# 192 tokens instead of 128 gather expert rows, and the first feed-forward layer runs in two passes

## The chip, the cores and the metric

One core of a Trainium2 chip runs the whole program. The metric is device time in microseconds (us) of one execution. The kernel before took 3000.18 us (median of three runs, 2999.29 to 3005.09). A difference of 0.2% is 6 us.

## What is computed

Two transformer layers on 512 tokens of width 1024, in float32. The parts that the change touches are the second half of the first layer and the first feed-forward layer of the second:

```
# product-key experts: 8 heads, each chooses 16 of 16384 experts per token
s1, i1 = top_k(scores of key half 1, 16);  s2, i2 = top_k(scores of key half 2, 16)
top_s, pos = top_k(s1[:, None] + s2[None, :], 16);  idx = (i1 * 128 + i2)[pos]
g = softmax(top_s)
act = gelu(einsum('thkd,td->thk', u_tab[idx], h))       # u_tab, v_tab: 16384 x 1024
x = x + einsum('thk,thkd->td', g * act, v_tab[idx])

# first feed-forward layer of the second block, 2816 hidden columns
x = x + 0.5 * ((silu(h2 @ w_gate) * (h2 @ w_up)) @ w_down)
```

Ahead of this stands an attention and recurrent block, behind it a second mixing block and a second feed-forward layer. Neither is changed.

## The kernel before

Activations lie transposed, channels on partitions and tokens along the free axis; `x` is eight tiles of 128 x 512. Every large product is made of three matmuls (`mm3`, lines 234 to 236): weights and activations are split into a high part in the fast float32 form and a low remainder, and high x high, low x high and high x low are added up in PSUM. A chunk of weights (128 x 1024, 512 KB) is loaded by SP into `wraw`, rounded by ScalarE into `whi` (L212), and subtracted by VectorE, or by GpSimd where `pool_lo` says so, into `wlo` (L213). One chunk feeds eight `mm3`, which is 24 matmuls.

`phase_b` computes the experts in two ways. The tokens 0 to `TG`-1 (128 before) gather the rows of the experts that they chose: GpSimd issues an indirect DMA for one row of every token (L884, 128 rows of 4 KB, 512 KB in one issue), and VectorE takes the dot product with the token's activations (`u` rows, L895) or adds the weighted row to an accumulator (`v` rows, L902). There are 128 choices per token and two tables, hence 256 such issues. The other `ND` tokens (384) go through all 16384 experts as products: 128 `u` tiles (`u_tile`, 8 `mm3` each), then 32 groups of `v` products (`v_group`, 4 chunks of 8 `mm3`), weighted by a dense table of gates that is zero where a token did not choose an expert.

The stages follow one another in time:

* **Routing** (`side`, `u_spill`). VectorE picks the best keys of each block of 128 tokens (`choose`, four times). For blocks 1 to 3 the gates of 4 tokens at a time are built: one-hot tiles `ohA`, `ohB` by VectorE, ScalarE and GpSimd (L852 to L863), a product per token (L838), a copy (L839), and a DMA to DRAM per 32 tokens. Beside this `SPILL` = 68 of the 128 `u` tiles are computed and spilled to DRAM.
* **Experts** (`main`). The other 60 `u` tiles and all `v` groups, with the gates (`gt`) and the spilled tiles (`gr`) read back, multiplied by VectorE or GpSimd in turn (L959), split (L962, L963), used, and the results added to `x` (L974).
* **First feed-forward layer** (`ffn`). 44 chunks up (gate and up columns for 22 hidden tiles) and 8 products of 22 `mm3` down, on all 512 tokens.

The generator `weave` sets the order: it emits a list `a` and beside it as much of a list `b` as a ratio of estimated costs allows; once `b` is done, a third list `c` may take its place. `u_spill` is woven with `side` (ratio `RR`), which emits the routing and with it `GR` parts of gather, and the gather itself is the third list. `main` is woven with the rest of the gather (ratio `VR`). Each gather issue and each use is held back (`pace`) until a matmul that stands ahead of it in that order is done, so the gather keeps step with TensorE. At most `ROWB`-1 = 3 rows are under way ahead of their use. Engines run their own queues in program order.

Of the kernel before, what the change touches and what calls it, by code (L numbers as in the profile page):

```python
# [25 lines left out]
C_IND, C_M1024, C_M128, C_M256, C_INVF, C_O256 = 832, 834, 835, 836, 837, 838  # L26
NCONST = 966
# [25 lines left out]
AR = 1.4        # paces: projections over attention, in both blocks  # L53
MR = 1.8
MO = 2          # query tile after which the memory's keys and values follow
SO = 0.5        # shift of the spilled groups among the others
BC = 1200       # cost of building the gates of 4 tokens
PJ = 15         # first expert tiles, whose low parts are left to Pool


def make_consts():
# [21 lines left out]
    c[:, C_O256:C_O256 + 128] = 1.0 / 256  # L83
    return c
# [33 lines left out]
class Norm:  # L118
# [33 lines left out]
    def finish(self, bc=True):  # L152
        k, nc = self.k, self.k.nc
        nb = self.n // 128
        ps = k.ps("st")
        for b in range(nb):
            nc.tensor.matmul(ps[:, b:b + 1], self.acc[:, b * 128:(b + 1) * 128], k.cst(C_M1024, 1),
                             start=True, stop=True)
        v = k.tiny.tile([128, nb], F32, name="nv")
        nc.vector.tensor_scalar(v, ps[:, :nb], EPS, None, op0=OP.add)  # L160
        self.rn = k.tiny.tile([128, nb], F32, name="nrn", bufs=3)
        k.rsqrt(v, self.rn)
        if bc:
            self.bc = k.tmp.tile([128, self.n], F32, name="nbc", bufs=2)
            pb = k.ps("T")
            for b in range(nb):
                nc.tensor.transpose(pb[:, b * 128:(b + 1) * 128], self.rn[:, b:b + 1].to_broadcast([128, 128]),
                                    k.ident)
            nc.scalar.activation(self.bc, pb[:, :self.n], AF.Copy)


class Kern:
# [44 lines left out]
    def pace(self, ins, back=1):  # L217
        """Hold ins, which is ready long before its turn, until a late matmul traced so far."""
# [4 lines left out]
    def flush(self):  # L223
        """What waits for the end of the last projection, traced some products into the next one."""
# [33 lines left out]
    def bcast_nat(self, f):  # L258
        """f(b) -> [128 tokens, 128] AP whose columns follow the output partitions."""
# [6 lines left out]
    # ------------------------------------------------------------------ setup  # L266
# [15 lines left out]
    def late_setup(self):  # L282
# [13 lines left out]
        # lambda of the differential attention  # L296
# [9 lines left out]
        # 4 * softplus(-rg_lambda)  # L306
# [20 lines left out]
    # ------------------------------------------------------------------ block 1  # L327
    def phase_a(self):
# [104 lines left out]
        # ---- differential attention  # L433
# [24 lines left out]
        def kq_pair(p):  # L458
            """Keys (normed) and raw queries of heads 2p, 2p+1; the queries' factors in FQ."""
# [196 lines left out]
        # ---- out projection and residual  # L656
# [22 lines left out]
    # ------------------------------------------------------------------ product-key experts  # L679
    # Tokens 0..TG-1 gather the rows of their experts; the others go through all experts as matrix  # L680
    # products, weighted by their gates (zero where a token did not choose an expert).
    def phase_b(self, n2):
        nc, I, x = self.nc, self.I, self.x
        ACT, V, G = nc.scalar, nc.vector, nc.gpsimd
        ND = T - TG
# [15 lines left out]
        hnat = gp_.tile([128, 1024], F32, name="hnat")  # L701
        hhi, hlo = [], []
        ph = None
        for hc in range(16):
# [9 lines left out]
            if hc % 2 == 1:  # L714
# [9 lines left out]
                if k % 4 == 0:  # L724
                    ph = self.ps("L")
                nc.tensor.transpose(ph[:, (k % 4) * 128:(k % 4) * 128 + 128], t[:, :TG], self.ident)
                if k % 4 == 3:
                    ACT.activation(hnat[:, (k // 4) * 512:(k // 4) * 512 + 512], ph, AF.Copy)
# [14 lines left out]
        gsel0 = gp_.tile([128, 8, 16], F32, name="gsel0")  # L743
        eidx = gp_.tile([128, 128], I32, name="eidx")

        eidx_done = []
# [36 lines left out]
            # position -> (r1, r2): the candidates run row by row, rows 0..7 of 16 // (r + 1), then ones  # L783
# [37 lines left out]
        def routing():  # L821
# [4 lines left out]
            for b in (1, 2, 3):  # L826
                gsel, sel = yield from choose(b)
                pt = self.ps("T")
# [6 lines left out]
                def build(stg, t0, t1, A, B):  # L835
# [5 lines left out]
                    if t1 == t0 + 28:  # L841
                        nc.sync.dma_start(Gd[(b - 1) * 4 + t0 // 32].rearrange("p j t -> p (j t)"),
                                          stg.rearrange("p j t -> p (j t)"))

                for t0 in range(0, 128, 32):
# [25 lines left out]
        def gather():  # L871
            """Tokens 0..127: dot products with the gathered rows of peer_u, then the weighted sum of peer_v's."""
            g2 = gsel0.rearrange("p h s -> p (h s)")
            acc = gp_.tile([128, 1024], F32, name="gacc")
            V.memset(acc, 0.0)
            dots = gp_.tile([128, 128], F32, name="dots")
            junk = gp_.tile([128, 1024], F32, name="junk")
            seq = [(tab, s) for s0 in range(0, 128, 16) for tab in "uv" for s in range(s0, s0 + 16)]
            rows = {}

            def issue(n):
                tab, s = seq[n]
                rows[n] = gp_.tile([128, 1024], F32, name="row", bufs=ROWB)
                self.pace(G.indirect_dma_start(out=rows[n], out_offset=None, in_=I[tab + "_nat"],  # L884
                                               in_offset=bass.IndirectOffsetOnAxis(ap=eidx[:, s:s + 1], axis=0)))

            for n in range(ROWB - 1):
                issue(n)
                yield 1170
            for n, (tab, s) in enumerate(seq):  # L890
                if n + ROWB - 1 < len(seq):
                    issue(n + ROWB - 1)
                row = rows.pop(n)
                if tab == "u":
                    self.pace(V.scalar_tensor_tensor(junk, row, 1.0, hnat, op0=OP.mult, op1=OP.mult,  # L895
# [7 lines left out]
                yield 1170  # L903
            for k in range(2):
                pt = self.ps("T")
                for q in range(4):
                    m = 4 * k + q
                    nc.tensor.transpose(pt[:, q * 128:(q + 1) * 128], acc[:, m * 128:(m + 1) * 128], self.ident)
                for q in range(4):
                    m = 4 * k + q  # L910
                    V.tensor_tensor(x[m][:, :TG], x[m][:, :TG], pt[:, q * 128:(q + 1) * 128], op=OP.add)
# [12 lines left out]
        def u_spill():  # L924
            for j in range(SPILL):
                yield from u_tile(j, rp, True)

        gat = gather()

        def side():  # L930
            c0 = c1 = 0.0
            for c in routing():
# [3 lines left out]
                while c1 < c0:  # L936
                    c = next(gat)
                    c1 += c
# [663 lines left out]
```

## Time and profile before

| | |
|---|---|
| median of three runs | 3000.18 us |
| lowest, highest | 2999.29, 3005.09 us |
| span of the profiled execution, first to last instruction | 2996.1 us |
| median above that span | 4.1 us |
| TensorE busy | 2865.3 us (96%) |
| VectorE, ScalarE, GpSimd busy | 2062.3, 1216.5, 822.9 us |
| bytes moved by DMA | 494.07 MB, 165 GB/s over the span |

The profiled execution has no time of its own beside its span; the fastest run lies 3.2 us above it. The table's shares are means over stages with different limits: the slices show a stretch in the middle, from slice 16 to 26, in which the DMA engines are at nine tenths, and a stretch from slice 10 on in which VectorE is.

### The profile page before, as it was taken

Reading aid. Unit: us, or ns where it says so; the run is one execution under the profiler, and the core shown is the slowest. Engines: PE = TensorE matmul, PEld = TensorE weight load, DVE = VectorE, ACT = ScalarE, POOL = GpSimd, SP = SyncE. Lnnn points to the kernel's source line nnn. Section 1 sums busy time; section 2 is a strip of 40 time slices with the busy share of each in tenths; the row PEclk is TensorE's granted clock in tenths of the full one; section 3 lists DMA queues with packets and bytes.
Section 4 is the critical chain, followed back from the end, with each engine's and each line's share of the span. In section 5 each row is a group of like instructions: output and inputs, shape, how many; then the busy total and the mean of one; then the engine's idle time right before and its main releaser. Section 6 shows DMA issues by size and latency. Waiting matters only on the chain. (4 is left out here: it accounts for less than half of the span.)

```text
span 2996.1 us, 39620 instructions
## 1 busy us (share of the span) xinstructions
PE 2865.3 (96%) x14551; PEld 2486.6 (83%) x14551; DVE 2062.3 (69%) x3978; ACT 1216.5 (41%) x1893; POOL 822.9 (27%) x633
## 2 busy tenths in 40 slices
PE   8899999999789998999999999999999999999999
PEld 6578777788789898899999999997888866678887
DVE  5763466679998967898898888995443477454432
ACT  4652344333365756333333333343222355632221
POOL 1320000000486968454544444520000022000000
PEclk9999999999999999999999999999999988999999
DMA  4123211332366767999998998962223321123232
GB/s 161 57 71 106 78 50 50 103 102 84 126 209 229 240 231 282 324 309 314 312 315 297 311 316 287 318 214 92 99 97 92 99 66 39 53 92 99 96 103 76
DMA packets 189250, 494.07 MB, mean 165 GB/s; under 512 B 16000, under 2 KB 84736, under 8 KB 187392
## 3 DMA queue, kind: packets, MB, share of 16 engines
q1 hardware_dynamic: 152192, 357.31, 35.8%
q0 software_dynamic: 36864, 134.23, 13.3%
q8 instruction: 115, 1.88, 0.3%
q14 instruction: 79, 0.65, 0.1%
HBM read 450.84 MB, written 40.63 MB: 164 GB/s over the span
## 5 line engine op out<-in xcount | busy, mean ns | idle before, releaser
L212 ACT ACTIVATE whi<-wraw 128x1024 fp32r<-128x1024 f32 (+1 forms) x526 | 547.2, 1041 | 1247.2 <-PE mm L235 600.1
L234 PE MATMUL mm<-hhi,whi 128*128 128x512 f32 (+1 forms) x2368 | 895.1, 378 | 30.1 <-ACT gs L918 17.0
L236 PE MATMUL mm<-hhi,wlo 128*128 128x512 f32 (+1 forms) x2368 | 882.1, 372 | 5.9 <-DVE wlo L213 5.8
L235 PE MATMUL mm<-hlo,whi 128*128 128x512 f32 (+1 forms) x2368 | 883.1, 373 | 0.0
L213 DVE TENSOR_TENSOR wlo<-wraw,whi 128x1024 fp32r<-128x1024 f32 (+1 forms) x491 | 605.9, 1235 | 274.6 <-ACT whi L212 272.4
L234 PEld LDWEIGHTS mm<-hhi,whi 128*128 128x128 f32 x2368 | 451.5, 191 | 89.7 <-ACT gs L918 17.9
L236 PEld LDWEIGHTS mm<-hhi,wlo 128*128 128x128 f32 x2368 | 451.0, 190 | 65.9 <-DVE wlo L213 9.6
L235 PEld LDWEIGHTS mm<-hlo,whi 128*128 128x128 f32 x2368 | 452.1, 191 | 53.3 <-issue 2.9
L884 POOL DMA_INDIRECT row<-v_nat,eidx x128 | 174.3, 1361 | 176.5 <-PE mm L236 47.6
L884 POOL DMA_INDIRECT row<-u_nat,eidx x128 | 169.3, 1323 | 160.0 <-PE mm L236 40.9
L863 POOL TENSOR_SCALAR ohB<-consts,sT 128x128 f32<-128x128 f32 x192 | 204.1, 1074 | 25.4 <-ACT sT L832 22.0
L902 DVE SCALAR_TENSOR_TENSOR gacc<-row,dots,gacc 128x1024 f32<-128x1024 f32 x128 | 173.8, 1358 | 14.3 <-PE mm L236 6.2
L895 DVE SCALAR_TENSOR_TENSOR junk<-row,hnat 128x1024 f32<-128x1024 f32 x128 | 165.0, 1289 | 17.6 <-DMA row<-u_nat,eidx 6.0
L213 POOL TENSOR_TENSOR wlo<-wraw,whi 128x1024 fp32r<-128x1024 f32 x35 | 89.2, 2549 | 320.1 <-ACT whi L212 319.8
L838 PE MATMUL L<-ohA,ohB 128*128 128x128 f32 x768 | 115.1, 283 | 25.1 <-POOL ohB L863 17.5
L234 PE MATMUL mm<-fhi,whi 128*128 128x512 f32 x352 | 139.1, 395 | 0.0
L236 PE MATMUL mm<-fhi,wlo 128*128 128x512 f32 x352 | 139.0, 395 | 0.0
L235 PE MATMUL mm<-flo,whi 128*128 128x512 f32 x352 | 139.0, 395 | 0.0
L838 PEld LDWEIGHTS L<-ohA,ohB 128*128 128x128 f32 x768 | 102.7, 192 | 37.1 <-POOL ohB L863 29.7
L1039 DVE TENSOR_TENSOR fu<-mm,nbc 128x512 f32<-128x512 f32 x44 | 30.4, 692 | 141.7 <-PE mm L236 141.7
L839 ACT ACTIVATE stg<-L 128x512 f32<-128x512 f32 x96 | 106.6, 1115 | 46.0 <-PE L L838 45.7
L1193 POOL MEMSET cvh<- 128x30 f32 x2 | 0.3, 126 | 382.8 <-DVE fu L1040 276.0
(2360 smaller groups left out, 5032.2 us busy)
## 6 DMA issues: line engine op xcount, KB each, us to landing
wraw<-u SPq DMA_DIRECT2D x128, 512.0 KB
wraw<-pv SPq DMA_DIRECT2D x128, 512.0 KB
gates<-stg SPq DMA_DIRECT2D x12, 2048.0 KB
gt<-gates SPq DMA_DIRECT2D x32, 768.0 KB
spill<-gs SPq DMA_DIRECT2D x68, 192.0 KB
gr<-spill SPq DMA_DIRECT2D x68, 192.0 KB
wraw<-w_f1g SPq DMA_DIRECT2D x22, 512.0 KB
wraw<-w_f1u SPq DMA_DIRECT2D x22, 512.0 KB
```

What stands on the lines that cost most here:

```text
L212: nc.scalar.activation(hi[:, :n], raw[:, :n], AF.Copy)
L213: (nc.gpsimd if pool_lo else nc.vector).tensor_tensor(lo[:, :n], raw[:, :n], hi[:, :n].bitcast(F32), op=OP.subtract)
L234: nc.tensor.matmul(ps, a[0], b[0], start=start, stop=False)
L235: nc.tensor.matmul(ps, a[0], b[1], start=False, stop=False)
L236: self.mms.append(nc.tensor.matmul(ps, a[1], b[0], start=False, stop=stop).ins.name)
L838: nc.tensor.matmul(gp[:, q * 128:(q + 1) * 128], B[:, q], A[:, q], start=True, stop=True)
L839: ACT.activation(stg[:, :, t1 - t0:t1 - t0 + 4].rearrange("p j t -> p t j"), gp.rearrange("p (t j) -> p t j", t=4), AF.Copy)
L863: G.tensor_scalar(B[:, q], iota, sT[:, 128 + tt:129 + tt], None, op0=OP.is_equal)
L884: self.pace(G.indirect_dma_start(out=rows[n], out_offset=None, in_=I[tab + "_nat"], in_offset=bass.IndirectOffsetOnAxis(ap=eidx[:, s:s + 1 ...
L895: self.pace(V.scalar_tensor_tensor(junk, row, 1.0, hnat, op0=OP.mult, op1=OP.mult, accum_out=dots[:, s:s + 1]), BACK)
L902: self.pace(V.scalar_tensor_tensor(acc, row, dots[:, s:s + 1], acc, op0=OP.mult, op1=OP.add), BACK)
L1039: V.tensor_tensor(u, pu, n.bc, op=OP.mult)
```

## The change

`TG` becomes 192. The first 128 gathering tokens are handled as before. The 64 others lie twice on the 128 partitions: the upper half of the partitions handles the choices 64 to 127 of the same tokens. So they need 64 choices x 2 tables = 128 further issues of 128 rows. Their activations (`hnat[1]`), expert numbers (`eidx1`) and gates (`gsel1`) are put there by small products, and the two halves of their result are added by a product with the stacked unit matrix `C_STK`. The products of `phase_b` then stream `ND` = 320 columns, not 384; ten, not twelve, blocks of 32 tokens get gates. 84 tiles are spilled, not 68. Once the routing has been emitted, the gather goes on beside the rest of `u_spill` at ratio `RR` = 1; what is left of it is spread evenly over the experts and over the up products of the first feed-forward layer.

That layer runs in two passes: `ffn_up` on the 320 tokens inside the weave, `ffn_down` on them, and then the whole layer again on the 192 gathering tokens, with all its weights loaded and split a second time. More low parts go to GpSimd: every third `u` tile after the spilled ones too, one chunk in eight of the `v` products, and every second `up` chunk of the two passes.

```diff
-SPILL = 68      # expert tiles whose activations wait in DRAM until the gates are there
-TG = 128        # tokens that gather their experts' rows
+SPILL = 84
+TG = 192
+TX = TG - 128
+XR = 128 // TX
+ND = T - TG
+MMC = 440
-VR = 0.345
+GC = 1170
...
-                    ph = self.ps("L")
-                nc.tensor.transpose(ph[:, (k % 4) * 128:(k % 4) * 128 + 128], t[:, :TG], self.ident)
+                    ph = [self.ps("L"), self.ps("L")]
+                ks = slice((k % 4) * 128, (k % 4) * 128 + 128)
+                nc.tensor.transpose(ph[0][:, ks], t[:, :128], self.ident)
+                for r in range(XR):
+                    nc.tensor.matmul(ph[1][r * TX:(r + 1) * TX, ks], t[:, 128:TG], self.ident, start=True, stop=True)
...
-                for t0 in range(0, 128, 32):
+                for t0 in range(TX if b == 1 else 0, 128, 32):
...
+            for i, (e, g, n) in enumerate(((eidx, gsel0.rearrange("p h s -> p (h s)"), 128), (eidx1, gsel1, TX))):
+                parts.append((e, g, hnat[i], gp_.tile([128, n], F32, name=f"dots{i}"), n))
...
-                    self.pace(V.scalar_tensor_tensor(junk, row, 1.0, hnat, op0=OP.mult, op1=OP.mult,
+                    self.pace(V.scalar_tensor_tensor(row, row, 1.0, hn, op0=OP.mult, op1=OP.mult,
...
-            yield from self.proj_g(ps, I["u"][j], hhi, hlo, n=ND, cost=490, pool_lo=spill and (j < PJ or j % 3 == 1))
-            g = pool.tile([128, ND], F32, name="gs", bufs=3 if spill else 2 * GS)
+            yield from self.proj_g(ps, I["u"][j], hhi, hlo, n=ND, cost=MMC, pool_lo=j < PJ or j % 3 == 1)
+            g = pool.tile([128, ND], F32, name="gs", bufs=2 if spill else 2 * GS)
...
-        weave(u_spill(), s_gen, RR, gat)
+        weave(u_spill(), s_gen, RR, counted(gat))
...
-                whi, wlo = self.wchunk(I["pv"][g, mp].rearrange("p m j d -> p (m j d)"), 1024)
+                whi, wlo = self.wchunk(I["pv"][g, mp].rearrange("p m j d -> p (m j d)"), 1024, mp == 1 and g % 2 == 1)
...
-        nf = Norm(self, "f1")
+        nf = Norm(self, "f1", n=ND)
...
-        weave(main(), gat, VR)
-        ev.close()
+            ev.close()
+            yield from self.ffn_up(ef, nf, "f1", MMC)
+
+        ef = ExitStack()
+        cost = ((128 - SPILL) * 9 + NG * GS * 8 + NKF * 16) * MMC
+        weave(main(), gat, left[0] / cost)
+
+        nb = Norm(self, "f1", n=TG)
+        self.ffn_down(ef, "f1", TG, lambda m: nb.add(m, x[m][:, :TG]))
         eg.close()
-        return nf
+        return nb
...
-    nf = k.phase_b(n2)
+    nb = k.phase_b(n2)
...
-    k.ffn(nf, "f1", nm, rt)
+    k.ffn(nb, "f1", lambda m: nm.add(m, k.x[m]), rt)
```

`ffn_up` and `ffn_down` are the two halves of the old `ffn`, on the number of tokens of the norm that they are given.

The order of the instructions moves in three places. GpSimd, at the end of the gate building (`ohB` are one-hot tiles, `row` the gathered rows, `gs` and `gr` activations that get their gates). Before:

```order
L863 TENSOR_SCALAR ohB<-consts,sT 128x128 x8
L884 DMA row<-u_nat,eidx 128x1024
L863 TENSOR_SCALAR ohB<-consts,sT 128x128 x4
L884 DMA row<-u_nat,eidx 128x1024 x2
L863 TENSOR_SCALAR ohB<-consts,sT 128x128 x4
L884 DMA row<-u_nat,eidx 128x1024 x3
L884 DMA row<-v_nat,eidx 128x1024 x2
L959 TENSOR_TENSOR gs<-gs,gt 128x384
```

and now:

```order
L889 TENSOR_SCALAR ohB<-consts,sT 128x128 x4
L220 TENSOR_TENSOR wlo<-wraw,whi 128x1024
L911 DMA row<-u_nat,eidx 128x1024 x11
L220 TENSOR_TENSOR wlo<-wraw,whi 128x1024
L911 DMA row<-v_nat,eidx 128x1024 x9
L220 TENSOR_TENSOR wlo<-wraw,whi 128x1024
L911 DMA row<-v_nat,eidx 128x1024 x7
L911 DMA row<-u_nat,eidx 128x1024 x3
```

Before, the first gated tile of the experts stands 5 rows behind the last one-hot tile. Now 48 gathered rows stand there, about three rows per spilled tile (GpSimd splits one such tile in three).

VectorE, in the up products of the first feed-forward layer (`fg`, `fu`: results of the gate and up columns; `flo`: low part of the hidden tile). Before:

```order
L213 TENSOR_TENSOR wlo<-wraw,whi 128x1024
L1044 TENSOR_TENSOR flo_18668<-fu,fhi_18667 128x512
L1035 TENSOR_TENSOR fg<-mm,nbc 128x512
L213 TENSOR_TENSOR wlo<-wraw,whi 128x1024
L1039 TENSOR_TENSOR fu<-mm,nbc 128x512
```

and now:

```order
L1092 TENSOR_TENSOR fg<-mm,nbc 128x320
L927 SCALAR_TENSOR_TENSOR row,dots_6734<-row,hnat_5091 128x1024
L220 TENSOR_TENSOR wlo<-wraw,whi 128x1024
L927 SCALAR_TENSOR_TENSOR row,dots_6734<-row,hnat_5091 128x1024
L1097 TENSOR_TENSOR fu<-mm,nbc 128x320
L220 TENSOR_TENSOR wlo<-wraw,whi 128x1024
L1098 TENSOR_TENSOR fu<-fu,fg 128x320
```

Gathered rows now stand among these. The last of the rows stands directly ahead of the first result of the down products.

SP, behind the down products (`w_f1g`, `w_f1u`, `w_f1d` are the layer's weights). Before, the last chunk of `w_f1d` was the last of the layer; now:

```order
L218 DMA wraw<-w_f1d 128x1024 x2
L218 DMA wraw<-w_f1d 128x768
L218 DMA wraw<-w_f1g 128x1024
L218 DMA wraw<-w_f1u 128x1024
L218 DMA wraw<-w_f1g 128x1024
L218 DMA wraw<-w_f1u 128x1024
```

The 68 loads of the layer stand there a second time.

## Rows read from the trace of the kernel before

**Rows 1.** The page: span, and the DMA engines' busy tenths in 40 slices.

```profile
span 2996.1 us, 39620 instructions
DMA  4123211332366767999998998962223321123232
```

**Rows 2.** Busy time of each engine by stage, granted clock, DMA share and rate.

```profile
core 0: us, PE busy (x) PEld busy (x) DVE busy (x) ACT busy (x) POOL busy (x), PEclk, DMA share, GB/s
860.00:935.00 75.00, 66.30 (x414) 63.42 (x413) 74.24 (x146) 49.60 (x87) 68.55 (x54) 0.95 0.72 240
935.00:1190.00 255.00, 238.86 (x1486) 230.34 (x1485) 198.70 (x359) 164.43 (x282) 203.26 (x172) 0.99 0.71 245
1190.00:1211.00 21.00, 15.37 (x87) 14.73 (x86) 7.00 (x10) 5.08 (x8) 4.20 (x5) 0.96 1.01 359
1211.00:2012.00 801.00, 780.91 (x4422) 770.94 (x4423) 720.96 (x960) 283.69 (x388) 375.85 (x272) 0.99 0.89 303
2012.00:2381.00 369.00, 366.32 (x1599) 299.79 (x1598) 165.09 (x214) 110.09 (x134) 0.25 (x2) 1.00 0.30 95
```

**Rows 3.** Timeline of TensorE: start, length; matmuls of 384, 512, 256 and 2 columns.

```profile
1500.03 0.33 PE L234 MATMUL L<-whi__13434,whi 128*128 128x384 f32 x1
...
1504.71 0.34 PE L234 MATMUL S<-whi__13419,whi 128*128 128x384 f32 x1
...
2200.03 0.39 PE L236 MATMUL mm<-hhi,wlo 128*128 128x512 f32 x1
...
2203.43 0.39 PE L236 MATMUL mm<-hhi,wlo 128*128 128x512 f32 x1
...
2484.33 0.28 PE L235 MATMUL mm<-mlo,whi 128*128 128x256 f32 x1
...
2485.51 0.28 PE L236 MATMUL mm<-mhi,wlo 128*128 128x256 f32 x1
...
435.02 1.05 PE L474 MATMUL st<-consts,sq 128*128 128x2 f32 x8 [0.24 <-ACT sq L470]
435.93 0.41 PE L537 MATMUL T<-consts,adiff 128*128 128x128 f32 x2
```

**Rows 4.** Groups of VectorE in the routing, 745 to 1200 us: busy, mean ns.

```profile
L862 DVE TENSOR_SCALAR ohA<-consts,sT 128x128 f32<-128x128 f32 x192 | 77.4, 464 | 7.6 <-PE L L838 6.6 <-ACT ohA L860 1.0
L852 DVE TENSOR_TENSOR ohA<-consts,sT 128x512 f32<-128x512 f32 x48 | 43.6, 909 | 11.3 <-PE L L838 11.3
L854 DVE TENSOR_TENSOR ohB<-consts,sT 128x512 f32<-128x512 f32 x48 | 36.6, 762 | 0.0
```

**Rows 5.** Groups of VectorE beside the experts, 1211 to 2012 us.

```profile
L213 DVE TENSOR_TENSOR wlo<-wraw,whi 128x1024 fp32r<-128x1024 f32 x185 | 237.4, 1285 | 16.9 <-ACT whi L212 15.3 <-issue 1.2
L902 DVE SCALAR_TENSOR_TENSOR gacc<-row,dots,gacc 128x1024 f32<-128x1024 f32 x112 | 152.6, 1362 | 12.5 <-PE mm L236 4.7 <-DMA row<-v_nat,eidx 3.1 <-issue 1.7
L895 DVE SCALAR_TENSOR_TENSOR junk<-row,hnat 128x1024 f32<-128x1024 f32 x97 | 126.8, 1307 | 10.8 <-PE L L236 4.7 <-DMA row<-u_nat,eidx 2.3 <-PE mm L236 1.5
L974 DVE TENSOR_TENSOR x<-x,L 128x384 f32<-128x384 f32 x127 | 69.5, 548 | 14.0 <-PE L L236 13.5
...
L911 DVE TENSOR_TENSOR x<-x,T 128x128 f32<-128x128 f32 x8 | 1.7, 275 | 0.0
```

**Rows 6.** Groups of GpSimd: in the routing, and beside the experts (1215 to 2013 us).

```profile
L213 POOL TENSOR_TENSOR wlo<-wraw,whi 128x1024 fp32r<-128x1024 f32 x31 | 78.8, 2541 | 71.1 <-ACT whi L212 70.9
...
L884 POOL DMA_INDIRECT row<-v_nat,eidx x109 | 151.1, 1387 | 166.7 <-PE S L236 44.0 <-PE mm L236 42.9 <-PE L L236 42.2
```

**Rows 7.** Timeline of VectorE in the routing: start, length.

```profile
803.74 0.28 DVE L798 TENSOR_TENSOR r<-r,rt 128x128 f32<-128x128 f32 x1
...
804.48 2.45 DVE L798 TENSOR_TENSOR r<-r,rt 128x128 f32<-128x128 f32 x1
```

**Rows 8.** Timeline of GpSimd at the same place.

```profile
804.27 2.52 POOL L213 TENSOR_TENSOR wlo<-wraw,whi 128x1024 fp32r<-128x1024 f32 x1 [4.60 <-ACT whi L212]
```

**Rows 9.** DMA share and rate at the program's start and in the feed-forward layer.

```profile
5.00:20.00 15.00, 9.51 (x28) 6.52 (x29) 11.26 (x21) 11.13 (x20) 1.84 (x2) 1.00 0.93 359
2030.00:2370.00 340.00, 340.00 (x1483) 278.68 (x1482) 146.02 (x174) 99.27 (x121) 0.25 (x2) 1.00 0.30 94
```

More of the change, by code (lines that the diff above doesn't have):

```diff
@@ L153, in finish @@
         k, nc = self.k, self.k.nc
-        nb = self.n // 128
+        offs = [b * 128 for b in range(self.n // 128)]
+        if self.n % 128:
+            offs.append(self.n - 128)
+        nb = len(offs)
         ps = k.ps("st")
-        for b in range(nb):
-            nc.tensor.matmul(ps[:, b:b + 1], self.acc[:, b * 128:(b + 1) * 128], k.cst(C_M1024, 1),
+        for b, o in enumerate(offs):
+            nc.tensor.matmul(ps[:, b:b + 1], self.acc[:, o:o + 128], k.cst(C_M1024, 1),
                              start=True, stop=True)
@@ L700, in phase_b @@
         idx = sp_.tile([128, 4, 16, 16], U32, name="idx")
-        hnat = gp_.tile([128, 1024], F32, name="hnat")
+        hnat = [gp_.tile([128, 1024], F32, name=f"hnat{i}") for i in range(2)]
         hhi, hlo = [], []
@@ L827, in routing @@
                 gsel, sel = yield from choose(b)
+                if b == 1:
+                    ef = rp.tile([128, 128], F32, name="pf")
+                    V.scalar_tensor_tensor(ef, sel[0], 128.0, sel[1], op0=OP.mult, op1=OP.add)
+                    px = self.ps("T")
+                    gf = gsel.rearrange("p h s -> p (h s)")
+                    for r in range(XR):
+                        for c, a in enumerate((ef, gf)):
+                            nc.tensor.matmul(px[r * TX:(r + 1) * TX, c * TX:(c + 1) * TX], self.ident[0:TX, 0:TX],
+                                             a[0:TX, r * TX:(r + 1) * TX], start=True, stop=True)
+                    V.tensor_copy(eidx1, px[:, 0:TX])
+                    V.tensor_copy(gsel1, px[:, TX:2 * TX])
+                    eidx_done.append(1)
+                    yield 600
                 pt = self.ps("T")
@@ L902, in gather, with add @@
                     self.pace(V.scalar_tensor_tensor(acc, row, dots[:, s:s + 1], acc, op0=OP.mult, op1=OP.add), BACK)
-                yield 1170
+                yield GC
+                if n == 255:
+                    yield from add(0, acc)
+            yield from add(1, acc)
+        def add(i, acc):
+            w = TX if i else 128
+            xs = slice(128, TG) if i else slice(0, 128)
             for k in range(2):
@@ L907, in gather @@
                     m = 4 * k + q
-                    nc.tensor.transpose(pt[:, q * 128:(q + 1) * 128], acc[:, m * 128:(m + 1) * 128], self.ident)
+                    if i:
+                        nc.tensor.matmul(pt[:, q * 128:q * 128 + w], acc[:, m * 128:(m + 1) * 128],
+                                         self.cst(C_STK, TX), start=True, stop=True)
+                    else:
+                        nc.tensor.transpose(pt[:, q * 128:(q + 1) * 128], acc[:, m * 128:(m + 1) * 128], self.ident)
                 for q in range(4):
                     m = 4 * k + q
-                    V.tensor_tensor(x[m][:, :TG], x[m][:, :TG], pt[:, q * 128:(q + 1) * 128], op=OP.add)
+                    V.tensor_tensor(x[m][:, xs], x[m][:, xs], pt[:, q * 128:q * 128 + w], op=OP.add)
                 yield 800
@@ L926, in u_spill, with counted @@
                 yield from u_tile(j, rp, True)
+        left = [(256 + 2 * TX + ROWB - 1) * GC + 3200]
+        def counted(g):
+            for c in g:
+                left[0] -= c
+                yield c
         gat = gather()
@@ L1029, in ffn, with ffn_up @@
+        self.ffn_down(ef, "f1", TG, lambda m: nb.add(m, x[m][:, :TG]))
+        eg.close()
+        return nb
+    def ffn_up(self, ef, n, pre, cost=650, side=None):
+        I = self.I
+        ACT, V = self.nc.scalar, self.nc.vector
         fp = ef.enter_context(self.pool("ffn", "right"))
+        w = n.n
         n.finish()
-        ahi, alo = [], []
+        self.fhid = []
         for f in range(NKF):
-            pg = self.proj(I[f"w_{pre}g"][f], n.hi, n.lo)
-            g = fp.tile([128, 512], F32, name="fg", bufs=2)
-            V.tensor_tensor(g, pg, n.bc, op=OP.mult)
+            pg, pu = None, None
+            pg = self.ps("mm")
+            yield from self.proj_g(pg, I[f"w_{pre}g"][f], n.hi, n.lo, n=w, cost=cost)
+            g = fp.tile([128, w], F32, name="fg", bufs=2)
+            V.tensor_tensor(g, pg[:, :w], n.bc, op=OP.mult)
@@ L1036, in ffn @@
             ACT.activation(g, g, AF.Silu)
-            pu = self.proj(I[f"w_{pre}u"][f], n.hi, n.lo)
-            u = fp.tile([128, 512], F32, name="fu", bufs=2)
-            V.tensor_tensor(u, pu, n.bc, op=OP.mult)
+            pu = self.ps("mm")
+            yield from self.proj_g(pu, I[f"w_{pre}u"][f], n.hi, n.lo, n=w, cost=cost, pool_lo=w < T and f % 2 == 1)
+            u = fp.tile([128, w], F32, name="fu", bufs=2)
+            V.tensor_tensor(u, pu[:, :w], n.bc, op=OP.mult)
             V.tensor_tensor(u, u, g, op=OP.mult)
-            a = fp.tile([128, 512], F32R, name=f"fhi{f}")
@@ L1049, in ffn @@
         for m in range(8):
-            ps = self.proj(I[f"w_{pre}d"][m], ahi, alo, nk=NKF)
-            V.scalar_tensor_tensor(x[m], ps, 0.5, x[m], op0=OP.mult, op1=OP.add)
-            if nxt is not None:
-                nxt.add(m, x[m])
-            else:
-                nc.sync.dma_start(self.out[:, m, :], x[m])
-        ef.close()
+            ps = self.proj(self.I[f"w_{pre}d"][m], hi, lo, nk=NKF, n=w)
+            xs = self.x[m][:, t0:t0 + w]
+            self.nc.vector.scalar_tensor_tensor(xs, ps[:, :w], 0.5, xs, op0=OP.mult, op1=OP.add)
@@ L1058, in rope_tables, with ffn @@
+            done(m)
+        ef.close()
+    def ffn(self, n, pre, done, side=None):
+        ef = ExitStack()
+        for _ in self.ffn_up(ef, n, pre, side=side):
+            pass
+        self.ffn_down(ef, pre, 0, done)
     def rope_tables(self):
```

65 lines of the change are left out of this document (34 added, 31 removed).

## Prediction

> **What bounds the kernel now.** I read the slices first, then the stages, then the groups inside a stage. The slices show the DMA engines at nine tenths in slices 16 to 26, and at two or three tenths in the feed-forward layers [rows 1]. The busy times by stage say more [rows 2]. From 860 to 935 us VectorE is busy 74.24 of 75 us: it sets the pace there, and it can run at 99%. While the gates are built (935 to 1190), TensorE is busy 94%. From 1190 to 1211, before the first gated product, TensorE waits a little and the DMA share is 1.01. Beside the experts (1211 to 2012) TensorE is busy 781 of 801 us and sets the time, but VectorE is at 90% and the DMA share is 0.89: neither has room for much. In the first feed-forward layer (2012 to 2381) TensorE is busy 99% and all else is slack. So the change takes work from the one engine that is full beside the experts, and gives it to two that are nearly full there. The granted clock is 0.99 to 1.00 in these stages, the upper level; I count no loss by it.
>
> **Prices.** A matmul's cost is the time between two starts [rows 3]: 15 intervals of 512 columns in 3.40 us, 0.227 each; 27 of 384 columns in 4.68, 0.173; 10 of 256 columns in 1.18, 0.118. 320 columns are halfway between the last two, 0.146. For 192 columns, the same slope (0.00043 us per column) gives 0.090. But eight matmuls of only 2 columns, with the same 128-column weight load, take 0.91 us, 0.114 each: there the load of the weights sets the pace. So 192 columns cost from 0.090 to 0.114, and I take 0.114, since each of them has a new weight too. For DMA, the stage of the experts gives 303 GB/s at a share of 0.89, hence 340 at full share; 1190 to 1211 gives 359/1.01 = 355 [rows 2]; the program's first microseconds 386, the feed-forward layer 313 [rows 9]. I take 340, from the stretch with the same mix of rows and chunks, and keep 313 and 386 as ends.
>
> **The change, part by part,** against the profiled execution; its span of 2996.1 us is 4.1 below the median of the runs, and I add these 4.1 at the end.
>
> *More turned activations.* 32 small products for `hnat[1]` at 0.114 us: +4.
>
> *Gates.* Ten blocks of 32 tokens, not twelve: 16 fewer builds. VectorE pays (77.4 + 43.6 + 36.6)/96 = 1.64 us a build where it builds alone [rows 4], so 16 save 26. In front of the last `choose`, where VectorE sets the pace, the order has 6 fewer gathered rows (1.32 us each) and 2 more low parts (1.29) come to -5: together -32. Beside the last 64 builds TensorE sets the pace; by the order, 40.5 `u` tiles of 24 x 0.173 = 4.16 us stood there and 45 of 24 x 0.146 = 3.50 stand there now: -11. The last gate is ready 43 us earlier.
>
> *A new tail of the routing.* Behind the last one-hot tile now stand 48 gathered rows and about 15 spilled tiles, ahead of the first gated product. Bytes: 48 x 0.524 MB, and 15 x (0.524 + 0.164), 35.5 MB: at 340 GB/s 104 us. TensorE needs 15 x 3.50 = 52 of these, VectorE 48 rows and 10 low parts, 78: both are hidden under the transfers.
>
> *Experts and up products,* one weave now. Bytes in MB: 299 rows 156.8, 44 `u` chunks 23.1, 128 of `v` 67.1, 44 of the up products 23.1, gates 32 x 0.655 = 21.0, spilled tiles 84 x 0.164 = 13.8: 304.9, or 897 us at 340 GB/s. TensorE: 1728 `mm3` x 3 x 0.146 = 755 us. VectorE: before, 721 busy. To this come 302 - 209 = 93 more row uses of 1.36 (+127), and 88 results of the up products of 0.48 (+42); 10 low parts of 1.285 leave (-13); 256 additions to `x` and 192 gatings and splits cost 0.48 instead of 0.548 (between 0.275 at 128 columns and 0.548 at 384), -30 [rows 5]. Sum 847.
>
> *Low parts on GpSimd.* 41 of them now fall in this stage, where there were none. GpSimd needs 2.54 us for one, VectorE 1.285 [rows 5, 6]. GpSimd has time for them: 302 row issues of 1.38, 41 low parts and 64 gatings are some 610 us. But the move isn't free for VectorE. In the routing, one operation of VectorE on 128 x 128 takes 0.28 us, and the next of the same line takes 2.45 [rows 7], and ends with the low part that GpSimd was at [rows 8]: an operation with two operands in SBUF stood still for 2.17 us. So a low part on GpSimd holds VectorE for between 0 (where it is at an operation with one operand) and 2.4 us. In this stage rows, low parts, gatings and splits have two such operands, about 85% of VectorE's time: 41 x 2.17 x 0.85 = 76 us. The Trainium skill states the same as a rule ("SBUF — State Buffer", the section on which engine contends: VectorE with two SBUF inputs and a GpSimd operation that reads SBUF lock one port pair, and the loser waits for the whole instruction); rows 7 and 8 agree with it in one place of the routing, and no row of before has it beside the experts for a low part. VectorE comes to 847 + 76 = 923 busy, at 99% 932 us, above the 897 of the transfers and the 755 of TensorE. At 932 us the DMA share would be 0.96.
>
> *The two passes.* The down products on 320 columns: 528 matmuls x 0.146 = 77. The second pass: 1584 x 0.114 = 181 (143 at 0.090). Ten us lie between products in this layer today (369 against 1584 x 0.227 = 359), and I keep them: 268 in place of 369. The 68 chunks loaded again are 34.6 MB, a third of what the transfers could move in that time, and GpSimd takes 11 of their low parts; TensorE hides both.
>
> **Sum.** Before, from the last gate on: 21 + 801 + 369 us. Now: 104 + 932 + 268, begun 43 - 4 = 39 us earlier. The 21 us ahead of the first gated product are transfers, and lie in the 104. So 1304 - 1191 - 39 = +74: a span of 3070, and a time of 3074 us. In short, the time moves by X - 962, where X is what the tail, the experts and the up products take: 1036 here. The forecast is slower, since VectorE and the DMA engines get more than TensorE gives back.
>
> **The rivals.** 0.2%, 6 us, is what a measurement of this kernel can tell from no change.
>
> *The transfers alone* (chance 0.18). If GpSimd's low parts fall in VectorE's gaps, the hold is near nothing, and X is 340.4 MB/340 = 1001: +39, 3039 us. For it: most of the 31 low parts of the routing leave VectorE's small operations alone for part of their time. Against: beside the experts VectorE has few gaps.
>
> *Faster* (0.24). One mechanism: DMA keeps up, and VectorE isn't held. At the rate of 1190 to 1211 us (359 GB/s) X is 948; at 386 GB/s the tail takes 92 and VectorE without the hold 847/0.99 = 856, again 948. Either way -14, 2986 us. It decides at 354 GB/s, where X is 962. For it: the 340 is read at a share below one, and a fuller queue may move more, as the program's start does. Against: the hold. Two figures of the Trainium skill would have it so ("DMA: Bandwidth & Descriptors", section on specifications: some 358 GB/s of HBM for a core, 435 for the fabric); the row of 1190 to 1211 is at the first, no long stretch of this trace is, and by 358 the transfers would need 951 us.
>
> *No change* (0.10). 354 to 359 GB/s, half of the hold, or a second pass at 0.090 us beside the transfers alone: X - 962 and the 38 us cancel. About 3000.
>
> *Waits that add up* (0.10). In VectorE's queue a row that lands late stops low parts, and so TensorE; with 3 rows ahead and two resources above 95% this recurs. In the stretch from 935 to 1190, where three engines are nearly full, TensorE loses 6% [rows 2]; 6% of 1036 is 62 more: 3136 us.
>
> That the change doesn't do what it says (rows left over after the up products, which the down products would wait for) has little chance: in the order the last row stands directly ahead of the first down result.
>
> **Numbers.** The forecast has 0.38, its own range 3045 to 3105 (a hold of 45 to 100 us). Slower by over 0.2%: 0.38 + 0.18 + 0.10 = 0.66; within 0.2%: 0.10; faster: 0.24. The range for 8 times in 10 reaches over the faster case to 2975 and to 3115.
>
> **What would show it.** Right: the last gate some 39 us earlier; then about 100 us at a DMA share near 1 and 340 GB/s with TensorE half idle; then a stage of some 930 us with VectorE at 98%, a DMA share of 0.96 and TensorE at 80 to 85%, waiting for low parts; VectorE's 128 x 1024 operations often 2 us longer where GpSimd is at a low part; the second pass at 0.114 us per matmul. Wrong: a rate above 354 GB/s over the stage; TensorE busy 95% there; VectorE's means unchanged; a tail that isn't there because GpSimd or the pace spread the 48 rows; a second pass bound by ScalarE or by loads.

## The result, and the profile after

The changed kernel takes 3156.8 us (median of four runs, 3151.3 to 3165.9) against 3001.8 (four runs of the kernel before): a ratio of 1.052, 95% interval 1.050 to 1.055. It is 155 us slower; the forecast was 74 slower, 3074 us, with a range from 2975 to 3115. The profiled executions differ by 154.1 us (spans of 3150.2 and 2996.1).

The slices of the changed kernel (page, part 2; to set beside [rows 1]; the first row is the granted clock):

```profile
PEclk9999999999899987899999999989999998999999
DMA  4123211323466778989899888878956641123332
```

The DMA engines are now at 0.7 to 0.9 from slice 15 to 28 (counted from 0), longer than before (0.8 to 0.9 from slice 16 to 25). The granted clock has a dip to 0.7 at slice 15, just behind the gates; before it was 0.96 to 1.00 from 935 to 2381 us [rows 2].

Busy times by stage (to set beside [rows 2]; columns as there). The stretches are: the tail behind the last gate, up to the last spilled tile; from there to the first gated product; experts and up products, to the first down product; the down products on 320 tokens and the start of the second pass; a further part of the second pass.

```profile
core 0: us, PE busy (x) PEld busy (x) DVE busy (x) ACT busy (x) POOL busy (x), PEclk, DMA share, GB/s
...
1156.00:1261.00 105.00, 60.06 (x339) 57.53 (x338) 66.37 (x72) 19.84 (x29) 60.08 (x45) 0.77 0.90 313
1261.00:1283.50 22.50, 15.16 (x86) 14.50 (x85) 16.58 (x21) 5.21 (x9) 15.02 (x11) 0.77 1.00 349
...
1283.50:2277.00 993.50, 834.85 (x5102) 795.76 (x5101) 884.29 (x1182) 318.89 (x453) 587.88 (x396) 0.94 0.87 300
2277.00:2365.00 88.00, 83.91 (x580) 83.24 (x578) 58.27 (x96) 31.86 (x46) 4.02 (x4) 1.00 0.60 188
...
2400.00:2540.00 140.00, 140.00 (x1256) 140.00 (x1255) 87.36 (x129) 72.64 (x100) 20.91 (x12) 1.00 0.67 196
```

The long stage is what matters: in 993.5 us TensorE is busy 84%, VectorE 89%, the DMA engines 87%, at 300 GB/s. No engine is full, where before TensorE was at 97%. The second pass is all TensorE.

Where the waiting is, in the view of the waits for that stage (engine, tile and line that waited; what it waited for; us in total, times, longest):

```profile
ACT whi L219 <- PE L L242: 188.6, 56, 9.7
ACT whi L219 <- DMA wraw<-pv: 113.0, 35, 7.8
...
ACT whi L219 <- DMA wraw<-u: 56.5, 18, 6.4
...
PE S L243 <- DVE wlo L220: 41.5, 30, 3.8
...
DVE row L927 <- DMA row<-u_nat,eidx: 23.6, 23, 2.5
...
DVE gacc L934 <- DMA row<-v_nat,eidx: 22.0, 17, 4.8
```

and, beside the experts before:

```profile
ACT whi L212 <- DMA wraw<-u: 9.1, 2, 4.7
```

ScalarE waits 170 us for weight chunks that land late (before, 9 us for those of `u`), VectorE 46 us for rows that land late (before, 5 us [rows 5]), and TensorE 42 us, in the row shown, for low parts from VectorE. A chunk's buffer in turn comes free only when its low part is made, so delays can go round in a circle.

VectorE's groups in the same stage (to set beside [rows 5]):

```profile
L220 DVE TENSOR_TENSOR wlo<-wraw,whi 128x1024 fp32r<-128x1024 f32 x171 | 224.8, 1322 | 1.1 <-ACT whi L219 1.0
L934 DVE SCALAR_TENSOR_TENSOR gacc<-row,dots,gacc 128x1024 f32<-128x1024 f32 x149 | 214.5, 1439 | 32.4 <-DMA row<-v_nat,eidx 22.0 <-PE L L243 4.4 <-PE mm L242 2.8
L927 DVE SCALAR_TENSOR_TENSOR row<-row,hnat 128x1024 f32<-128x1024 f32 x144 | 203.0, 1413 | 36.0 <-DMA row<-u_nat,eidx 23.6 <-PE mm L243 8.3 <-PE L L243 1.9
L1025 DVE TENSOR_TENSOR x<-x,S 128x320 f32<-128x320 f32 x128 | 61.6, 481 | 19.3 <-PE S L243 18.8
```

The means went up (1285 to 1322 ns, 1362 to 1439, 1307 to 1413) although the shapes are the same. One such place, in the timeline of VectorE:

```profile
1697.37 3.33 DVE L927 SCALAR_TENSOR_TENSOR row<-row,hnat 128x1024 f32<-128x1024 f32 x1 [1.87 <-DMA row<-u_nat,eidx]
...
1702.17 1.21 DVE L927 SCALAR_TENSOR_TENSOR row<-row,hnat 128x1024 f32<-128x1024 f32 x1
```

and in that of GpSimd:

```profile
1697.26 2.36 POOL L220 TENSOR_TENSOR wlo<-wraw,whi 128x1024 fp32r<-128x1024 f32 x1
```

The first of the two row operations waits for its row, starts just behind a low part on GpSimd, and takes 2.12 us more than the second. GpSimd is done at 1699.62, and the row operation ends 1.08 us behind that: it stood until GpSimd was done, as in [rows 7, 8].

### The profile page after: what moved, and what is told of

Its sections match the earlier page's. It is cut to its first block, busy times and chain, and to the rows that moved or that the text cites. A ratio compares the mean times of both kernels' runs of the same rounds, so it can differ in the third digit from the quotient of the medians.

```text
span 3150.2 us, 43780 instructions
## 1 busy us (share of the span) xinstructions
PE 2823.9 (90%) x16066; PEld 2478.9 (79%) x16066; DVE 2279.1 (72%) x4271; ACT 1257.1 (40%) x1984; POOL 1105.4 (35%) x787
## 5 line engine op out<-in xcount | busy, mean ns | idle before, releaser
L241 PE MATMUL mm<-hhi,whi 128*128 128x320 f32 (+2 forms) x2720 | 946.2, 348 | 65.3 <-ACT gs L961 29.4
L243 PE MATMUL mm<-hhi,wlo 128*128 128x320 f32 (+2 forms) x2720 | 936.0, 345 | 64.7 <-POOL wlo L220 51.2
L242 PE MATMUL mm<-hlo,whi 128*128 128x320 f32 (+2 forms) x2720 | 932.0, 343 | 0.0
L220 POOL TENSOR_TENSOR wlo<-wraw,whi 128x1024 fp32r<-128x1024 f32 x93 | 240.3, 2584 | 494.1 <-ACT whi L219 486.3
L927 DVE SCALAR_TENSOR_TENSOR row<-row,hnat 128x1024 f32<-128x1024 f32 x192 | 268.5, 1402 | 65.9 <-DMA row<-u_nat,eidx 46.5
L243 PE MATMUL mm<-fhi,wlo 128*128 128x320 f32 (+2 forms) x528 | 172.0, 326 | 0.9 <-DVE wlo L220 0.9
L242 PE MATMUL mm<-flo,whi 128*128 128x320 f32 (+2 forms) x528 | 172.2, 326 | 0.0
L241 PE MATMUL mm<-fhi,whi 128*128 128x320 f32 (+2 forms) x528 | 171.8, 325 | 0.0
L243 PEld LDWEIGHTS mm<-fhi,wlo 128*128 128x128 f32 x528 | 99.7, 189 | 9.2 <-DVE wlo L220 1.1
L242 PEld LDWEIGHTS mm<-flo,whi 128*128 128x128 f32 x528 | 99.7, 189 | 8.1
```

The costliest lines, as they stand in the source:

```text
L220: (nc.gpsimd if pool_lo else nc.vector).tensor_tensor(lo[:, :n], raw[:, :n], hi[:, :n].bitcast(F32), op=OP.subtract)
L241: nc.tensor.matmul(ps, a[0], b[0], start=start, stop=False)
L242: nc.tensor.matmul(ps, a[0], b[1], start=False, stop=False)
L243: self.mms.append(nc.tensor.matmul(ps, a[1], b[0], start=False, stop=stop).ins.name)
L927: self.pace(V.scalar_tensor_tensor(row, row, 1.0, hn, op0=OP.mult, op1=OP.mult, accum_out=dots[:, s:s + 1]), BACK)
```

## The experiments

The question was why the long stage takes 994 us, where the sum had put VectorE at 932 and the transfers at 897. "The stage" is from the first gated product to the first down product, in the profiled execution. E1, E2, E3, E8 and E9 are single runs, E5 and E6 have two each, the others four.

**Three runs that take one load away.** E1 leaves VectorE 32 of the 1024 columns of each row:

```diff
+                cc = slice(0, 32 if late else 1024)
...
-                    self.pace(V.scalar_tensor_tensor(row, row, 1.0, hn, op0=OP.mult, op1=OP.mult,
+                    self.pace(V.scalar_tensor_tensor(row[:, cc], row[:, cc], 1.0, hn[:, cc], op0=OP.mult, op1=OP.mult,
```

(and the same at the weighted sum). E2 issues no rows and lets VectorE work on one fixed row, filled once (the products of the `u` rows go to a second tile); E3 does both:

```diff
             def issue(n):
+                if late:
...
+                    rows[n] = late[1]
+                    return
```

E1: 

> Left out: from the first gated product on, VectorE works on 32 of the 1024 columns of each gathered row. All transfers stay. The stage from the first gated product to the first down product took 994 us in the changed kernel. Theory T1 (the transfers set the pace, and with three chunks and three rows under way they give 300 to 313 GB/s, not 340): 304.9 MB need 974 to 1016 us, the stage stays at 960 or more. T2 (VectorE, with GpSimd's hold, sets the pace): VectorE loses some 293 x 1.35 = 395 of its 884 busy us, the stage falls to the 897 us of the transfers at 340 GB/s or below. T3 (it is waits of each for the other, none alone): between, 900 to 960.

E2: 

> Left out: from the first gated product on, no row is gathered (no transfer, no issue on GpSimd); VectorE does its full work on one fixed row instead. T1: 148 MB are left, no bound; the stage falls to what VectorE needs, 850 to 900 us. T2: VectorE's 884 us at 99% stay, 890 or more, and what GpSimd's issues held of it goes: 870 to 930. T3: 870 to 930. If the rows' transfers cost little the stage stays above 960, which would speak against T1.

E3: 

> Left out: from the first gated product on, both the rows' transfers and all but 32 of VectorE's 1024 columns per row. All theories: the stage is TensorE's, 5184 matmuls x 0.146 = 755 us and some 10 to 30 of gaps, 765 to 790, and the granted clock goes from 0.94 back to 0.99. A stage above 820 would name another bound: weight chunks, ScalarE or GpSimd's low parts.

The times were 3058.2, 3070.8 and 2944.6 us, the stages 896, 915 and 787. Busy times of E1 in that stage:

```profile
1281.00:2177.00 896.00, 799.66 (x5106) 780.12 (x5106) 581.48 (x1186) 320.93 (x455) 508.35 (x398) 0.95 0.94 334
```

of E2:

```profile
1280.00:2195.00 915.00, 813.85 (x5105) 781.55 (x5104) 875.03 (x1184) 318.52 (x452) 207.43 (x104) 0.95 0.50 158
```

and of E3:

```profile
1283.00:2070.00 787.00, 761.01 (x5105) 752.00 (x5104) 568.92 (x1187) 319.64 (x453) 174.20 (x103) 1.00 0.58 184
```

With VectorE eased, the same bytes go through at 334 GB/s: T1, which had 300 to 313 as all that these buffers give, falls. By the numbers set down, both runs fit T2, and E1 is 4 us below what T3 had. But T2 can't explain 994 us for 884 of work: in E2 VectorE does the same work, 875, in 79 us less, and all that was taken away is the rows' coming and their issues. So neither sets the time alone. With either load eased the stage is done in 896 to 915 us; together they take 80 to 100 more. E3 gives TensorE's own price, 761 busy in 787, with the clock back at 1.00.

**E4: the low parts back on VectorE** (three places; in the second pass too).

```diff
-            yield from self.proj_g(ps, I["u"][j], hhi, hlo, n=ND, cost=MMC, pool_lo=j < PJ or j % 3 == 1)
+            yield from self.proj_g(ps, I["u"][j], hhi, hlo, n=ND, cost=MMC, pool_lo=spill and (j < PJ or j % 3 == 1))
...
-                whi, wlo = self.wchunk(I["pv"][g, mp].rearrange("p m j d -> p (m j d)"), 1024, mp == 1 and g % 2 == 1)
+                whi, wlo = self.wchunk(I["pv"][g, mp].rearrange("p m j d -> p (m j d)"), 1024)
...
-            yield from self.proj_g(pu, I[f"w_{pre}u"][f], n.hi, n.lo, n=w, cost=cost, pool_lo=w < T and f % 2 == 1)
+            yield from self.proj_g(pu, I[f"w_{pre}u"][f], n.hi, n.lo, n=w, cost=cost)
```

> The 41 low parts of the stage (and 11 of the second pass) go back from GpSimd to VectorE. T1: no change within 15 us of the changed kernel's 3157. T2: VectorE gains 41 x 1.95 us of hold and pays 41 x 1.29, 27 us less, and the products that waited for a low part on GpSimd come sooner: 20 to 50 us less, 3107 to 3137. If GpSimd's low parts did relieve VectorE as if there were no hold: 40 us or more slower, 3197.

3141.9 us, 15 less than the changed kernel (the runs of the two don't overlap), which is at the edge of what T1 allowed and below the 20 to 50 of T2, and against the 40 more that GpSimd's relief without a hold would have meant; ratio to the kernel before 1.046 (1.043 to 1.050). VectorE does 41 low parts more, and yet is busy less, 852 us against 884. The stage of E4, its two row groups, and what ScalarE waited for chunks there:

```profile
1278.00:2263.00 985.00, 838.17 (x5103) 794.93 (x5104) 851.59 (x1228) 321.22 (x455) 468.49 (x359) 0.94 0.89 304
...
L934 DVE SCALAR_TENSOR_TENSOR gacc<-row,dots,gacc 128x1024 f32<-128x1024 f32 x151 | 201.7, 1336 | 31.3 <-DMA row<-v_nat,eidx 24.6 <-PE mm L243 2.9 <-PE S L243 2.0
L927 DVE SCALAR_TENSOR_TENSOR row<-row,hnat 128x1024 f32<-128x1024 f32 x144 | 177.6, 1236 | 34.2 <-DMA row<-u_nat,eidx 22.7 <-PE L L243 4.4 <-PE mm L243 3.5
...
ACT whi L219 <- DMA wraw<-pv: 186.4, 62, 9.0
...
ACT whi L219 <- DMA wraw<-u: 41.5, 16, 6.2
```

So each low part that was given to GpSimd cost VectorE more than it saved: a relief that was a load. But the stage fell by 9 us only, to 985: VectorE still waits 47 us for rows, and ScalarE now 228 us for chunks, where it was 170.

**E5 to E7: deeper buffers beside the gated products.** E5 has three more row buffers, E6 three more for weight chunks, E7 two more of each. (The first two parts of the diff are E5's, the last is E6's.)

```diff
-                rows[n] = gp_.tile([128, 1024], F32, name="row", bufs=ROWB)
+                if sum(p is gp_ for p, _ in rows.values()) < ROWB:
+                    rows[n] = gp_, gp_.tile([128, 1024], F32, name="row", bufs=ROWB)
+                else:
+                    rows[n] = late[0], late[0].tile([128, 1024], F32, name="rowx", bufs=3)
...
-                if n + ROWB - 1 < len(seq):
-                    issue(n + ROWB - 1)
+                for _ in range(2):
+                    if nxt < len(seq) and nxt < n + ROWB + (3 if late else 0):
+                        issue(nxt)
+                        nxt += 1
...
-        raw = self.wp.tile([128, 1024], F32, name="wraw", bufs=RAWB)
+        if getattr(self, "wx", None) is not None and self.nraw % 6 >= RAWB:
+            raw = self.wx.tile([128, 1024], F32, name="wrawx", bufs=3)
+        else:
+            raw = self.wp.tile([128, 1024], F32, name="wraw", bufs=RAWB)
```

E5: 

> Nothing is left out. Beside the gated products up to 6 gathered rows are under way ahead of their use, not 3 (three more buffers). So far: VectorE without its row work leaves a stage of 896 us, transfers without rows one of 915, both together 994. Theory C1 (the 80 to 100 us are waits of two nearly full queues for each other, and shallow buffers pass each delay on): the waits of VectorE for rows, 45 us, go, the stage falls by 30 to 60 us to 935 to 965, the time to 3095 to 3125. Theory C2 (transfers and VectorE slow each other whatever the depth, by memory ports or by GpSimd's issues): the stage stays within 12 us of 994.

E6: 

> Nothing is left out. Beside the gated products six buffers of weight chunks, not three. C1: ScalarE's waits for chunks (113 and 57 us in the changed kernel) go for the most part, the stage falls by 30 to 60 us to 935 to 965. C2: within 12 us of 994. C3 (more chunks under way only take the bandwidth from the rows): VectorE's waits for rows grow above 45 us and the stage is 990 or more.

E7: 

> Nothing is left out. Two more buffers for rows and two more for chunks beside the gated products. C1: the stage comes within 30 us of the larger of the two alone, 915 to 945, the time 3078 to 3108. C2: within 12 us of 994.

E5: 3133.2 us, stage 972; E6: 3156.8, stage 998; E7: 3121.2, ratio 1.040 (1.038 to 1.042), stage 961. The stage of E5 and VectorE's waits for rows there:

```profile
1285.00:2256.70 971.70, 837.39 (x5109) 802.47 (x5107) 895.55 (x1184) 319.85 (x454) 580.72 (x395) 0.93 0.89 307
...
DVE row L933 <- DMA row<-u_nat,eidx: 4.7, 4, 1.5
DVE gacc L940 <- DMA row<-v_nat,eidx: 3.6, 4, 1.2
```

and waits of E6:

```profile
ACT whi L223 <- PE L L246: 341.0, 98, 12.1
...
DVE gacc L938 <- DMA row<-v_nat,eidx: 25.1, 16, 4.4
DVE row L931 <- DMA row<-u_nat,eidx: 24.3, 16, 3.6
```

In E5 the waits for rows fall from 46 us to 8, as C1 has it, but the stage by 22, less than the 30 to 60 of C1 and more than the 12 of C2. E6 gains nothing: ScalarE hardly waits for `u` and `v` chunks any more, it waits for TensorE instead (341 us for 189), and VectorE's waits for rows are 49 us for 46. This fits C3, but also C2; C2 falls by E5 and E7. So C1 holds in part: row buffers count, and chunk buffers add some 10 us once rows are on time. E7's 961 is still 46 above the stage of E2.

**E8: 68 spilled tiles**, as before, so that no tail stands behind the last gate (`SPILL = 68`).

> Nothing is left out. 68 tiles are spilled as before, so some 15 tiles fewer stand behind the last gate; most of the 48 rows of the tail and those tiles go into the stage. If only sums count (TensorE 755 + 52, VectorE 884 + 78, transfers 335 MB): the tail goes from 105 to under 30 us and the stage grows by 70 to 85, so 3127 to 3152. If a tail with TensorE half idle were worth as much as the stage: 3157 within 10. If a longer coupled stage loses more than the tail: above 3167.

3164.1 us, inside the spread of the changed kernel's own runs and within the 10 of its second number. From the last gate to the first gated product it took 24 us instead of 127, and the stage grew by 116, to 1110. So time in the tail was worth about as much as time in the stage: its half-idle TensorE is not a loss by itself, and the sums, which had 5 to 30 us less, miss here too.

**E9: half of VectorE's row work** (`512 if late`, as in E1).

> Left out: from the first gated product on, VectorE works on 512 of the 1024 columns of each gathered row; all transfers stay. VectorE's busy time in the stage falls from 884 to about 690, 70% of it. If the loss comes only where both queues are nearly full: the stage is that of the transfers, 896 to 910, as with 32 columns. If VectorE's load counts in proportion at any level (0.25 us of stage per us of VectorE, from 994 - 896 over 395): 945.

3092.1 us, stage 925:

```profile
1283.50:2208.00 924.50, 810.55 (x5106) 789.00 (x5106) 726.40 (x1184) 319.72 (x453) 529.55 (x397) 0.94 0.91 323
```

VectorE is at 79% (726 us, not the 690 expected). Neither number of the two: the loss over the 896 of E1 is 29 us here, and 98 with VectorE at 89%. It falls faster than the load, but is not yet nothing.

**E10 and E11: both remedies.** E10 is E7 with E4's edit. In E11 the gatings leave GpSimd too:

```diff
-                (G if q % 2 else V).tensor_tensor(s3, s3, gt[:, :, q, :], op=OP.mult)
+                V.tensor_tensor(s3, s3, gt[:, :, q, :], op=OP.mult)
```

E10: 

> Nothing is left out. Two more buffers for rows and chunks, and the low parts back on VectorE. Alone they gave 33 and 9 us of the stage. If they add up: stage 950, time 3107. If VectorE's freed 32 us count in full now that rows and chunks come on time: stage 930, time 3087. If the deep buffers already hid the hold: stage 961 within 8.

E11: 

> Nothing is left out. As the run before, and VectorE also does the 62 gatings that GpSimd had, so that beside the gated products GpSimd only issues rows. In the changed kernel a gating on GpSimd held VectorE for 0.64 us in the mean, and one on VectorE takes 0.5 to 0.6: VectorE's load stays within 10 us. If only that counts: within 10 us of the run before. If row issues that queue behind gatings, which wait for spilled tiles, made rows late: 10 to 25 us less.

E10: 3071.7 us, ratio 1.023 (1.020 to 1.026); E11: 3068.2, 1.021 (1.017 to 1.025). Stage of E7:

```profile
1282.00:2243.00 961.00, 828.15 (x5105) 793.63 (x5104) 886.82 (x1184) 320.18 (x456) 588.71 (x397) 0.94 0.89 309
```

of E10:

```profile
1286.00:2191.00 905.00, 808.75 (x5109) 771.78 (x5109) 847.62 (x1224) 320.52 (x453) 483.58 (x356) 0.97 0.92 328
```

and of E11:

```profile
1290.00:2184.00 894.00, 807.61 (x5112) 777.42 (x5111) 846.15 (x1290) 322.15 (x453) 388.98 (x292) 0.96 0.94 333
```

The low parts, worth 9 us of the stage alone, are worth 56 once rows and chunks have buffers (961 to 905), more than any number expected. VectorE's busy time gives 39 of these (887 to 848); in E7 TensorE also waited 25 us for low parts from GpSimd, which E10 doesn't have. How the 56 divide isn't shown. E11's stage is 11 us shorter than E10's, but the times of the two overlap, within the 10 us of its first number.

In E11 the stage is 894, what it was in E1 with VectorE eased (896, 334 GB/s), and VectorE's waits for rows are 5 us:

```profile
DVE gacc L944 <- DMA row<-v_nat,eidx: 2.6, 3, 1.7
...
DVE row L937 <- DMA row<-u_nat,eidx: 1.9, 2, 1.0
```

So the 100 us are gone, with every byte and every product in place: 33 by the buffers, 56 more by the low parts, and the last 11 with the gatings, if they are more than noise. GpSimd still issues every row in E11, so the issues, which E2 took away together with the transfers, aren't what cost them.

Even so E11 is 2% slower than the kernel before. To win, the tail, the experts and the up products had to fit into 962 us, 354 GB/s by the sum, and no run held more than 334 over the stage. That the rest is the transfers is likely, not shown: E1, with VectorE at 65%, is no faster than E11, but E1 has the shallow buffers, and E1's edit with the deep ones was not run. No version here that does all the work beats the kernel before.

## Why the prediction was wrong

The direction was right, the size half of what came. Point by point, from the profiled executions (+154.1 measured, +74 forecast):

* **Gates.** Forecast 39 us earlier; the DMA of the last ones was issued at 1156.0 instead of 1190.5, 34 earlier. 5 us.
* **Tail.** 104 forecast, 104.9 measured (1156.0 to 1260.9). That it fits so well is luck: 32.9 MB moved, not 35.5, at 313 GB/s and a share of 0.90, not at 340 and 1, and the two misses cancel. TensorE was half idle (57%) as forecast, and waited 37 us there for low parts from GpSimd.
* **The 21 us ahead of the first gated product** were put into the tail; they came behind it (1260.9 to 1283.5). The gates and spilled tiles are read only after the last tile is spilled. TensorE works on up to 15 us there, and the transfers run at 1.00, so this stretch belongs to the long stage: 1016.7 us from the last spill to the first down product, against 932.
* **The long stage: the step that failed.** It came 85 us longer than forecast; the sum was 80 short, since gates (+5), tail (+1), the passes (-5) and all that follows (-5) nearly cancel. The prediction said: "VectorE comes to 847 + 76 = 923 busy, at 99% 932 us, above the 897 of the transfers and the 755 of TensorE", and took the largest as the time. It put the waits between VectorE and the transfers at nothing (and at 62 us in a rival). Counted like the 932, from the last spill on, the largest by itself was right: E2, without the rows, takes 934 us and E1, with VectorE eased, 916, for 932 and 897 forecast. Both loads together take 1017. What failed is the largest-of-three. The 99% was read where VectorE waits for hardly anyone ([rows 2], 860 to 935). In the long stage its queue also waits for rows that a nearly full set of DMA engines brings, with three ahead; it was busy for 884.3 + 16.6 = 901 us of 1017, 89%. Deeper buffers alone gave back 33 us of it (E7); the rest came back only when GpSimd's low parts went too (E10, E11).
* **Inside VectorE's 901** two misses cancel in part: the hold was some 8 us more than forecast (next point), its own work some 30 us less than the 847.
* **The clock** was put at no loss, from "0.99 to 1.00 in these stages"; [rows 2] has 0.95 and 0.96 in two of them. Here it was 0.94 in the long stage, and with it TensorE was busy for 835 + 15 = 850 us there, not 755. That this set the time isn't shown (last section).
* **GpSimd's hold on VectorE.** 76 us forecast for 41 low parts, 1.85 each. Taking them off GpSimd lowered VectorE's busy time by 32 us although it then did 41 x 1.28 = 52 of work more: 84 us, 2.05 each. The mechanism and its size in VectorE's busy time were right; what it cost the stage was 9 us alone and up to 56 behind deeper buffers (E4, E10).
* **The second pass.** 0.114 us per matmul forecast; measured 0.112, as the timeline of TensorE shows from the first to the last of 19 starts (2.01 us over 18 intervals):

```profile
2450.02 0.27 PE L241 MATMUL mm<-hhi,whi 128*128 128x192 f32 x1
...
2452.03 0.27 PE L241 MATMUL mm<-hhi,whi 128*128 128x192 f32 x1
```

  320 columns: 0.146, as forecast. Down products and second pass took 263 us (2277.6 to 2540.8) for 268.

**The rivals.** "Waits that add up" is what happened. It was given 0.10 and priced at 6%, 62 us, from a stretch (935 to 1190) where only TensorE's loss was read, and where VectorE was at 78% and GpSimd at 80% [rows 2], not nearly full; it cost 85, 9%, and E1, E2 and E11 show it. "The transfers alone" (3039 us) needed VectorE out of the way: E1 and E11 come nearest, at 3058 and 3068. "Faster" needed 354 GB/s over the stage; 334 was reached, and only without the mutual waits. "No change" needed that too, or half of the hold, or a second pass at 0.090; the hold came in full and the pass at 0.112. The 358 GB/s for a core that the Trainium skill states ("DMA: Bandwidth & Descriptors", specifications) were held over no long stretch: 359 for 21 us of the kernel before [rows 2], 349 from 1261 to 1283.5 here, 300 over the long stage, and 334 in the best of the runs. Its rule on the port that VectorE and GpSimd lock ("SBUF — State Buffer") agrees with E4, beside the experts too.

## What to carry to other kernels

When two resources that feed each other both come out above nine tenths, the time need not be the larger of the two: price the waits between them, or ask what buffers stand between. Here the stage took 896 to 915 us with either load eased, and 994 with both and three rows ahead; with five ahead and VectorE not held it was 894, at 95% of VectorE and a DMA share of 0.94.

Work moved to an idle engine is no relief if it holds the busy one meanwhile: 41 low parts on GpSimd cost VectorE 84 us and saved it 52. A remedy that does little alone can do much with another (9 us and 33 us alone, 89 together), so a small result of one edit doesn't settle its cause.

## What was not expected of the hardware

* TensorE's granted clock (a mean over its two levels, 1.2 and 2.4 GHz) was lower in the stretches where TensorE stood idle between products: 0.77 in the tail (60 us busy of 105) and 0.94 in the long stage (835 of 994); in E3 (761 of 787) it was 1.00. The same matmuls made TensorE busy for 835 us in the changed kernel and 761 in E3. That this set the time isn't shown: E11's stage, at 0.96 and 808 us busy, is as short as E1's with VectorE eased.
* The rate of the DMA engines at a given share was not constant. The stage before gave 303 GB/s at 0.89, 340 at full share; E11 moves 333 at 0.94 and E1 334 at 0.94, 355 at full share; the tail's 313 at 0.90 is 348. What was out of reach in the changed kernel is the full share itself: of its stretches shown here only the 22 us ahead of the first gated product held 1.00. Why the rate per share rises with the load stays open.
